# Two transformer blocks on one core: Silu gates taken together, keys and gated rows turned by DMA, softmax shifts formed in the maximum's own instruction

## The chip, the core and the metric

The kernel runs on one core of a Trainium2 chip. The core has a matrix engine (PE; its weight loads are listed as PEld), three engines for elementwise work (DVE, ACT, POOL), a queue engine (SP) that issues most DMAs, and 16 DMA engines. Each engine works through its own list in order, and waits on semaphores where an entry needs another engine's result. The metric is the device time of one execution in microseconds.

## The reference, cut to what matters

512 tokens of width 1024 pass through two blocks. In the second block 256 context rows give further keys and values.

```
# block 1
x = x + diff_attention(rmsnorm(x))      # 8 heads, two softmaxes each: p = softmax(s0) - lam*softmax(s1),
                                        # s = q.k - slope_h*distance, causal; 64 wide, q and k rms-normalised
x = x + hier_moe(rmsnorm(x))            # 16 experts, two per token inside one of four groups
# block 2
p = modulated_norm(x) @ w_in            # f_in, f_gate, q, k, v, na_gate: 512 columns each
y = real(fft2(f_in.reshape(512, 4, 128), axes=(tokens, channels))) / sqrt(512*128)
f = (y @ w_four) * silu(f_gate)
s = concat(q.k/8 + bias where the key is in the query's window, q.kc/8)     # kc: 256 context keys
n = softmax(s) @ concat(v, vc) * silu(na_gate)                              # q, k, kc rms-normalised, with gains
out = x + gate * (concat(f, n) @ w_out)
```

## The kernel before

Every product is done in fp16 as a high and a low part: `hilo` (L165) makes them, the high part by a Copy on ACT, the low one by a subtraction on DVE, and `mm3` (L155 in the rows) issues three matmuls for each product. Work on tokens is in four tiles of 128 rows. Apart from a start that is ordered by hand, a scheduler takes the program's instructions by priority (roughly: as written) as soon as its own model has their inputs ready, and so fixes each engine's list at build time. Buffers come from pools: eight PSUM banks (three "mm", two "tp", three "sc"), 18 large SBUF slots, five 1024-wide work buffers (`w4`), six 512-wide ones (`w2`).

The span has these stages (us from its start): 0 to 60 loads and the first norm; 60 to 262 projections and attention of block 1; 262 to 300 output projection and router; 300 to 580 the sixteen experts; 580 to 640 the context rows and block 2's norm; 640 to 712 the products of block 2 for k, v, q and the attention's gate (kx, vx, qx, ng), one after the other; 712 to 840 the neighbourhood attention with the Fourier branch between its pieces; 837 to 875 the product with w_out (z).

**Softmax, both blocks.** Scores of one query tile and head stand in a PSUM bank (s, ns). One DVE instruction adds the bias and reduces to the row's maximum (L508, L1423); a small DVE instruction multiplies the maximum by minus the scale (nmx L511: 64 times; nmxn L1426: 32 times); ACT takes Exp with that as its bias (L512, L1427).

**Turning.** Keys and queries are needed with channels on the partitions. `pairs_T` (L299) turns them by PE: transposes against the identity (L217, fp32) into a "tp" bank, then `hilo` with the gain. It does so for the context's keys (bank kcp, 8 transposes) and block 2's keys (kxp, 16), both called between the four products of vx, by `late.pop()`. Probabilities of the neighbourhood attention (`flip`) are split in SBUF and turned by `dma_start_transpose` on SP (L1436): 32 of them, from one half of two ring buffers to the other. SP takes DMAs in its list's order; an entry that waits holds all behind it.

**The Fourier branch.** `fourier()` (L1285) is a generator that `neighbours` advances at two points of each of its steps: `Fill(fourier(), 72)`. It computes u for the groups g = 0..3 (f_in, turned), folds each by DVE into f and fh/fl, multiplies by cosines and sines over the channels (`first(g)`: bank ab, evacuated to the tiles ab), then over the tokens (yp, yq: both "mm" banks), unfolds into yT, and then, tile by tile, the gate's product fg, its Silu, and `fouriered(t)`: y @ w_four (fo), times the gate (DVE, in fg), four transposes (fT) into cT. `first(g)` runs after the product u of g+1; `first(3)` right before the loop over yp and yq. The weights of w_out (bo) are loaded late in this branch. The attention's own turned result (nT) goes to the other half of cT.

Of the kernel before, what the change touches and what calls it, by code (L numbers as in the profile page):

```python
# [10 lines left out]
F16 = mybir.dt.float16  # L11
# [89 lines left out]
def block_kernel(ctx: ExitStack, tc: tile.TileContext, a, out, dbg=None):  # L101
# [74 lines left out]
    def S(name, i=0, n=1):  # L176
        lo = COLS[name][0]
        return sm[:, lo + i:lo + i + n]
# [140 lines left out]
    def proj_heads(ah, al, n, w, gain, th, tl, desc, nm, nxt, every, late, done=None, dense=False, pop=1):  # L319
        nats = []  # L320
        scale = []
        for t in range(n):
            if t % 2 == 0:
                pair = w4(f"{nm}nat{t}")
            nat = pair[:, (t % 2) * 512:(t % 2) * 512 + 512]
            ps = done[t] if done else (yield from project(ah, al, t, w.w, f"{nm}{t}", every=every, dense=dense, then=scale))
            while scale:
                scale.pop()()
            if t == pop and late:
                yield from late.pop()  # L330
            scale.append(heads_norm(ps, nat, f"{nm}{t}", desc))
            if nxt:
                nxt.piece(-(-4 // n))
            nats.append(nat)
            yield
        scale.pop()()
        late.append(pairs_T(nats, gain, th, tl, nm))
# [98 lines left out]
    nc.vector.tensor_scalar_mul(g2, S("q2g", 0, 2), 16.0)  # L436
    wog = const.tile([P, 1], F32, name="wog")
# [38 lines left out]
    def attention(hf, fill, last=None):  # L476
# [19 lines left out]
        def soft1(h, i):  # L496
            head = hf * 4 + h
            hsc = 2.0 ** -(head + 1) / MASTER0
            n = P * (i + 1)
            nm = f"{head}{i}"  # L500
            if i == 0:
                sums_h[h] = tiny.tile([P, 2, 4], F32, tag="sums", name="sums" + nm)
            sums = sums_h[h]
            pex = []
            for c, ps in enumerate(st[h, i]):
                z = w2(f"z{nm}{c}")
                mx = tiny.tile([P, 1], F32, tag="mx", name=f"mx{nm}{c}")
                nc.vector.tensor_tensor_reduce(out=z[:, :n], in0=ps[:, :n], in1=master[:, 384 - P * i:],  # L508
                                               scale=1.0, scalar=-3e38, op0=ALU.add, op1=ALU.max, accum_out=mx)
                nmx = tiny.tile([P, 1], F32, tag="nmx", name=f"nmx{nm}{c}")  # L510
                nc.vector.tensor_scalar(nmx, mx, -hsc, None, op0=ALU.mult)  # L511
                nc.scalar.activation(z[:, :n], z[:, :n], AF.Exp, bias=nmx, scale=hsc, accum_out=sums[:, c, i:i + 1])  # L512
                pex.append(z)
            st[h, i] = pex
# [705 lines left out]
    for f in kcn:  # L1220
        f()
# [9 lines left out]
    late.append(pairs_T([cnat[:, :512], cnat[:, 512:]], lambda j: g2[:, 1:2], kch, kcl, "kc"))  # L1231
# [4 lines left out]
    run_all(proj_heads(xh, xl, NT, W["k"], lambda j: g2[:, 1:2], kxh, kxl, D2, "kx", None, KD, late, None, True, 3))  # L1236
# [9 lines left out]
    for i, b in enumerate((1, 2, 3, 0)):  # L1246
        ps = bank("sc" if i % 2 else "mm", f"vx{b}")
        vw = W["v"].w
        for k in range(KD):
            bh, bl = (v[:, k, :] for v in xw) if b == 0 else (v[:, k, 128 * b - 64:128 * b + 64] for v in (xh, xl))  # L1250
            mm3(ps, bh, bl, vw[0][:, k, :], vw[1][:, k, :], k == 0, k == KD - 1)
        if i == 0:
            run_all(late.pop())
        hilo(vxh[:, b, :], vxl[:, b, :], ps, 1.0 / SW)
        W["q"].piece()
# [14 lines left out]
    _, cTh, cTl = hl_slots("cT")  # L1270
# [4 lines left out]
    def fourier():  # L1275
# [51 lines left out]
        yield from first(3)  # L1327
# [7 lines left out]
        for g in range(4):  # L1335
            pp_, pq = bank("mm", f"yp{g}"), bank("mm", f"yq{g}")
# [23 lines left out]
        def fouriered(t):  # L1360
# [6 lines left out]
            stt(fg[:, 512:], ps, D2, fg[:, :512], op1=ALU.mult)  # L1367
            yield
            pt = bank("tp", f"fT{t}")
            for k in range(4):  # L1370
                transpose_to(pt[:, k * P:(k + 1) * P], fg[:, 512 + k * P:512 + (k + 1) * P])
            hilo(cTh[:, 0:4, s], cTl[:, 0:4, s], pt.rearrange("p (k t) -> p k t", k=4), 4.0)

        for t in range(NT):
            ps = yield from project(xh, xl, t, W["fg"].w, f"fg{t}", every=2)
            fos[t] = w4(f"fg{t}")
            nc.scalar.activation(fos[t][:, :512], ps, AF.Silu, scale=D2)
            f4.piece()
            if t == NT - 1:
                W["o0"] = Weights(cols(a["w_out"], 0), "bo0")  # L1380
            yield
            if t > 0:
                yield from fouriered(t - 1)
        W["o0"].piece(2)
        yield from fouriered(3)
        W["o0"].piece(2)

# [3 lines left out]
    def neighbours(fill):  # L1391
# [15 lines left out]
        def soft(j, t):  # L1407
# [7 lines left out]
            for c in range(2):  # L1415
                nm = f"n{j}{t}{c}"
                m = nbm[c]
                if t != 2:
# [4 lines left out]
                nc.vector.tensor_tensor_reduce(out=z, in0=st[j, t][c], in1=m, scale=1.0, scalar=-3e38, op0=ALU.add,  # L1423
                                               op1=ALU.max, accum_out=mx)
                nmx = tiny.tile([P, 1], F32, tag="nmx", name="nmx" + nm)
                nc.vector.tensor_scalar(nmx, mx, -ISC, None, op0=ALU.mult)  # L1426
                nc.scalar.activation(z, z, AF.Exp, bias=nmx, scale=ISC, accum_out=sums[:, 2 * t + c:2 * t + c + 1])  # L1427
# [134 lines left out]
```

## Time and profile before

| | us |
|---|---|
| median of 3 runs | 874.3 (873.94, 874.3, 877.48) |
| profiled execution | 876.94 |
| its span on the engines | 875.1 |
| busy in the span: PE / DVE / ACT / POOL | 806.9 / 644.7 / 523.9 / 145.8 |
| mean granted PE clock (1 is full speed) | 0.971 |

PE is busy for 92% of the span, DVE for 74%, ACT for 60%. These are averages over stages of different kinds, and a busy PE is not PE at its peak. The profiled execution lies 1.84 us above its own span and 2.64 us above the median of the runs.

### The profile page before, as it was taken

What the parts mean: (1) busy time and instruction counts of PE and PEld (TensorE: products, weight loads), DVE (VectorE), ACT (ScalarE), POOL (GpSimd) and SP (SyncE); (2) the same over time, 40 slices, a digit from 0 to 9 for tenths busy, and PEclk for the clock granted to TensorE, in tenths of its full rate; (3) what the DMA queues carried; (4) which work ended last, traced back from release to release, by engine and by line L of the source; (5) the groups of instructions that cost most, each with busy time, mean ns of one, the idle gap of its engine ahead of it and who ended that gap; (6) DMA issues with size and microseconds to landing.
All of it is one profiled execution on the core that took longest, in us unless ns stands there. A gap on an engine that the chain in (4) does not pass through costs nothing. (4 is left out here: it accounts for less than half of the span.)

```text
span 875.1 us, 19152 instructions
## 1 busy us (share of the span) xinstructions
PE 806.9 (92%) x7986; PEld 509.6 (58%) x7986; DVE 644.7 (74%) x1204; ACT 523.9 (60%) x847; POOL 145.8 (17%) x130
## 2 busy tenths in 40 slices
PE   5999989999989799999999999889799999899998
PEld 3444445444435688788887887654454445544544
DVE  5756667677994798999999999947945347886732
ACT  6525435454773388888888869755343246687600
POOL 1240122000152400000000000016440203221000
PEclk9999999999999699999999999989899999899999
DMA  9964330446127569999999999917900018559712
GB/s 340 387 224 137 123 97 25 144 147 238 49 82 280 191 220 344 375 400 395 394 398 397 394 398 380 373 33 256 357 13 24 1 27 179 110 107 231 187 44 71
DMA packets 108043, 187.62 MB, mean 214 GB/s; under 512 B 37199, under 2 KB 37712, under 8 KB 107952
## 3 DMA queue, kind: packets, MB, share of 16 engines
q1 hardware_dynamic: 102176, 167.61, 56.3%
q0 software_dynamic: 3568, 12.45, 4.0%
q10 hardware_dynamic: 2208, 6.29, 1.8%
q8 instruction: 64, 1.05, 0.5%
q14 instruction: 27, 0.22, 0.1%
HBM read 165.37 MB, written 12.58 MB: 203 GB/s over the span
## 5 line engine op out<-in xcount | busy, mean ns | idle before, releaser
L155 PEld LDWEIGHTS <-hT 128*128 128x128 f16 x576 | 55.2, 99 | 66.6 <-issue 8.6
L155 PEld LDWEIGHTS <-xnT 128*128 128x128 f16 x456 | 44.8, 99 | 52.9 <-issue 4.7
L155 PEld LDWEIGHTS <-hx 128*96 128x96 f16 x384 | 47.0, 125 | 33.9 <-issue 2.2
L512 ACT ACTIVATE z<-z,nmx 128x128 f32<-128x128 f32 (+3 forms) x64 | 35.6, 557 | 46.3 <-DVE nmx L511 46.1
L955 POOL DMA_DIRECT2D y_d<-y x16 | 8.2, 513 | 262.0 <-ACT y L954 262.0
L155 PE MATMUL xgp<-se,XSh 128*128 128x96 f16 x512 | 48.3, 211 | 0.9 <-DVE se L886 0.9
L155 PE MATMUL xgp<-se,XSl 128*128 128x96 f16 x512 | 48.5, 211 | 0.2 <-issue 0.2
L155 PEld LDWEIGHTS <-XSh 128*128 128x128 f16 x512 | 45.6, 101 | 1.3 <-DVE se L886 1.0
L155 PEld LDWEIGHTS <-XSl 128*128 128x128 f16 x512 | 45.7, 101 | 0.3 <-issue 0.3
L508 DVE CUSTOM_DVE_ANT_0 z<-s,misc_a 128x128 f32<-128x128 f32 (+3 forms) x64 | 30.1, 481 | 4.7 <-PE s L155 4.5
L1420 POOL TENSOR_TENSOR late_b<-late_b,misc_b 128x256 f32<-128x256 f32 x24 | 19.3, 823 | 82.5 <-DVE mxn L1423 82.2
L155 PEld LDWEIGHTS <-cT 128*128 128x128 f16 x216 | 20.1, 99 | 20.5 <-DVE cT L163 0.4
L163 DVE SCALAR_TENSOR_TENSOR ring<-zn,ring 128x512 f16<-128x512 f32 x32 | 22.0, 711 | 12.0 <-ACT ring L1428 12.0
L1423 DVE CUSTOM_DVE_ANT_0 zn<-ns,late_b 128x512 f32<-128x512 f32 x32 | 21.0, 682 | 12.2 <-PE ns L155 11.7
L1427 ACT ACTIVATE zn<-zn,nmxn 128x512 f32<-128x512 f32 x32 | 22.8, 714 | 11.3 <-DVE nmxn L1426 11.3
L155 PEld LDWEIGHTS <-oT 128*128 128x128 f16 x192 | 17.6, 100 | 18.0 <-issue 2.0
L155 PE MATMUL y<-wo0s,oT 128*128 128x512 f16 x96 | 26.1, 380 | 0.7 <-DVE on L564 0.3
L155 PE MATMUL s<-kk,qk 64*128 64x128 f16 (+3 forms) x192 | 25.6, 300 | 0.1
L155 PE MATMUL y<-wo1s,oT 128*128 128x512 f16 x96 | 24.2, 394 | 1.2 <-ACT oT L166 0.7
L155 PE MATMUL k<-wk1s,hT 128*128 128x512 f16 x96 | 23.3, 380 | 1.6 <-DVE nmx L511 1.6
L166 ACT ACTIVATE pth<-pt 128x128 f16<-128x128 f32 (+3 forms) x32 | 13.7, 429 | 17.8 <-PE pt L217 17.7
L155 PE MATMUL v<-wv1s,hT 128*128 128x512 f16 x96 | 24.3, 394 | 0.0
(734 smaller groups left out, 2385.0 us busy)
## 6 DMA issues: line engine op xcount, KB each, us to landing
w_gate<-in_w_gate SPq DMA_DIRECT2D x32, 1024.0 KB, 11.5
w_up<-in_w_up SPq DMA_DIRECT2D x32, 1024.0 KB, 11.1
w_down<-in_w_down SPq DMA_DIRECT2D x32, 1024.0 KB, 12.0
ada<-in_w_ada SPq DMA_DIRECT2D x12, 1024.0 KB, 7.4
y_d<-y POOLq DMA_DIRECT2D x16, 384.0 KB, 6.7
wk<-in_da_w_in SPq DMA_DIRECT2D x4, 1024.0 KB, 13.5
wv<-in_da_w_in SPq DMA_DIRECT2D x4, 1024.0 KB, 10.0
wo<-in_da_w_out SPq DMA_DIRECT2D x4, 1024.0 KB, 7.0
```

The costliest lines, as they stand in the source:

```text
L155: nc.tensor.matmul(o, lhsT=lhsT, rhs=rhs, start=start, stop=stop)
L163: return nc.vector.scalar_tensor_tensor(o, in0, sc, in1, op0=op0, op1=op1)
L166: nc.scalar.activation(h, src, AF.Copy, scale=scale)
L508: nc.vector.tensor_tensor_reduce(out=z[:, :n], in0=ps[:, :n], in1=master[:, 384 - P * i:], scale=1.0, scalar=-3e38, op0=ALU.add, op1=ALU.m ...
L512: nc.scalar.activation(z[:, :n], z[:, :n], AF.Exp, bias=nmx, scale=hsc, accum_out=sums[:, c, i:i + 1])
L955: nc.gpsimd.dma_start(y_d[e * CAP:(e + 1) * CAP, :], y[:CAP, :])
L1420: nc.gpsimd.tensor_tensor(m[:, :256], pos[j, "b"][:, c * 256:(c + 1) * 256], mask[:, v:v + 256], op=ALU.add)
L1423: nc.vector.tensor_tensor_reduce(out=z, in0=st[j, t][c], in1=m, scale=1.0, scalar=-3e38, op0=ALU.add, op1=ALU.max, accum_out=mx)
L1427: nc.scalar.activation(z, z, AF.Exp, bias=nmx, scale=ISC, accum_out=sums[:, 2 * t + c:2 * t + c + 1])
```

## The change

Three edits go together.

1. *Softmax.* The reducing instruction multiplies by minus the scale and takes the minimum, so that it leaves the negated, scaled scores and their minimum, which is Exp's bias as it stands; Exp runs with scale -1. The 64 nmx and the 32 nmxn fall away.
2. *Keys of block 2.* The context's keys and the block's keys are normalised, split in SBUF (times 64) and turned by DMA: six DMA transposes on SP (2 of kcsp, 4 of the kxnat buffers) for 24 PE transposes and the eight evacuations of their banks. The k gain is multiplied into the q gain.
3. *Fourier branch.* `first(3)` is called after g = 1 of the loop over yp and yq. The four gate products are evacuated by a Copy; four Silus from SBUF are written after all of them, then `fouriered` for the four tiles. It splits the gated rows in SBUF and turns them by DMA into cT (4 DMA transposes on SP) instead of 16 PE transposes. The first half of w_out's weights is asked for after the fourth gate product is evacuated.

```
+    def turn(norm, nat, s, o):
+        def go():
+            norm()
+            hilo(s[:, :512], s[:, 512:], nat, 64.0)
+            nc.sync.dma_start_transpose(o, s)
+        return go
...
             scale.append(heads_norm(ps, nat, f"{nm}{t}", desc))
+            if turned is not None:
+                scale.append(turn(scale.pop(), nat, pair[:, 512:].bitcast(F16), turned[:, :, t * P:(t + 1) * P]))
...
-        late.append(pairs_T(nats, gain, th, tl, nm))
+        if turned is None:
+            late.append(pairs_T(nats, gain, th, tl, nm))
...
+    nc.vector.tensor_scalar(g2[:, 0:1], g2[:, 0:1], g2[:, 1:2], 1.0 / 64.0, op0=ALU.mult, op1=ALU.mult)
...
-                                               scale=1.0, scalar=-3e38, op0=ALU.add, op1=ALU.max, accum_out=mx)
-                nmx = tiny.tile([P, 1], F32, tag="nmx", name=f"nmx{nm}{c}")
-                nc.vector.tensor_scalar(nmx, mx, -hsc, None, op0=ALU.mult)
-                nc.scalar.activation(z[:, :n], z[:, :n], AF.Exp, bias=nmx, scale=hsc, accum_out=sums[:, c, i:i + 1])
+                                               scale=-hsc, scalar=3e38, op0=ALU.add, op1=ALU.min, accum_out=mx)
+                nc.scalar.activation(z[:, :n], z[:, :n], AF.Exp, bias=mx, scale=-1.0, accum_out=sums[:, c, i:i + 1])
...
-    for f in kcn:
-        f()
+    csp = w4("kcsp", F16)
+    for t, f in enumerate(kcn):
+        turn(f, cnat[:, t * 512:(t + 1) * 512], csp[:, t * 1024:(t + 1) * 1024],
+             kvc16[:, :2048].rearrange("p (m t) -> p m t", m=8)[:, :, t * P:(t + 1) * P])()
...
-    late.append(pairs_T([cnat[:, :512], cnat[:, 512:]], lambda j: g2[:, 1:2], kch, kcl, "kc"))
...
-        if i == 0:
-            run_all(late.pop())
         hilo(vxh[:, b, :], vxl[:, b, :], ps, 1.0 / SW)
...
-        yield from first(3)
...
         for g in range(4):
+            if g == 2:
+                yield from first(3)
             pp_, pq = bank("mm", f"yp{g}"), bank("mm", f"yq{g}")
...
             stt(fg[:, 512:], ps, D2, fg[:, :512], op1=ALU.mult)
+            src = fg[:, :512].bitcast(F16)
+            hilo(src[:, :512], src[:, 512:], fg[:, 512:], 4.0)
+            nc.sync.dma_start_transpose(cT[0].rearrange("p v k t -> p (v k) t")[:, :, s], src)
             yield
-            pt = bank("tp", f"fT{t}")
-            for k in range(4):
-                transpose_to(pt[:, k * P:(k + 1) * P], fg[:, 512 + k * P:512 + (k + 1) * P])
-            hilo(cTh[:, 0:4, s], cTl[:, 0:4, s], pt.rearrange("p (k t) -> p k t", k=4), 4.0)
...
-            nc.scalar.activation(fos[t][:, :512], ps, AF.Silu, scale=D2)
+            nc.scalar.activation(fos[t][:, :512], ps, AF.Copy, scale=D2)
             f4.piece()
-            if t == NT - 1:
-                W["o0"] = Weights(cols(a["w_out"], 0), "bo0")
             yield
-            if t > 0:
-                yield from fouriered(t - 1)
-        W["o0"].piece(2)
-        yield from fouriered(3)
-        W["o0"].piece(2)
+        W["o0"] = Weights(cols(a["w_out"], 0), "bo0")
+        for t in range(NT):
+            nc.scalar.activation(fos[t][:, :512], fos[t][:, :512], AF.Silu)
+        for t in range(NT):
+            yield from fouriered(t)
+            W["o0"].piece(1)
```

The scheduler decides what becomes of this on each engine. Three places follow; the numbers behind the names are buffers.

PE of the kernel before, where the scores (ns) of one attention step give way to the Fourier branch and `first(3)` comes next:

```order
L155 LDWEIGHTS qkx
L155 MATMUL ns_10658<-kvc,qkx 128x256
L155 LDWEIGHTS fh_10557
L155 MATMUL ab_10565<-late_b,fh_10557 128x128
L155 LDWEIGHTS fh_10557
L155 MATMUL ab_10565<-late_b,fh_10557 128x128
L155 LDWEIGHTS fh_10557
L155 MATMUL nyp_10578<-late_b,fh_10557 1x128
```

PE of the change at the same place, behind the same scores:

```order
L155 LDWEIGHTS qkx
L155 MATMUL ns_10358<-kvc,qkx 128x256
L155 LDWEIGHTS ab_9869
L155 MATMUL yp_10394<-dfts,ab_9869 128x257
L155 LDWEIGHTS ab_9869
L155 MATMUL yp_10394<-dfts,ab_9869 128x257
L155 LDWEIGHTS ab_9870
L155 MATMUL yp_10394<-dfts,ab_9870 128x257
L155 LDWEIGHTS ab_9869
L155 MATMUL yq_10395<-dfts,ab_9869 128x256
```

Where PE had the matmuls on fh, the last folded group, yp and yq of the first groups now stand, whose input is ab.

ACT of the kernel before, around the first gate Silu:

```order
L1427 ACTIVATE zn_10875,nsum_10865<-zn_10875,nmxn_10878 128x512
L1377 ACT_TABLE_LOAD
L1377 ACTIVATE fg_10927<-fg_10884 128x512
L1428 ACTIVATE ring_9997<-zn_10875 128x512
L1427 ACT_TABLE_LOAD
L1427 ACTIVATE zn_10957,nsum_10865<-zn_10957,nmxn_10960 128x512
```

ACT of the change, from the first gate's Copy (L1387) to the second's; Silu is L1392, Exp L1434, the Copy into the ring L1435:

```order
L1387 ACTIVATE fg_10737<-fg_10694 128x512
L1434 ACTIVATE zn_10767,nsum_10679<-zn_10767,mxn_10768 128x512
L1392 ACT_TABLE_LOAD
L1392 ACTIVATE fg_10737<-fg_10737 128x512
L1435 ACTIVATE ring_9844<-zn_10767 128x512
L1434 ACT_TABLE_LOAD
L1434 ACTIVATE zn_10773,nsum_10679<-zn_10773,mxn_10774 128x512
L1434 ACTIVATE zn_10857,nsum_10679<-zn_10857,mxn_10858 128x512
L1435 ACTIVATE ring_9844<-zn_10773 128x512
L1387 ACTIVATE fg_10821<-fg_10778 128x512
```

The first Silu stands between two Exps, with a table load on either side, ahead of the second gate's Copy. The whole list holds 15 table loads in either kernel.

SP of the change, late in the neighbourhood attention (L1381 turns the gated rows, L1443 the probabilities, L195 loads weights, L1501 loads the residual rows); the kernel before has no L1381 entry, and its bo loads stand further up among the ring's:

```order
L1443 DMA_TRANSPOSE ring_9843<-ring_9843 128x8x128
L1381 DMA_TRANSPOSE cT_9840<-fg_10737 128x8x128
L1443 DMA_TRANSPOSE ring_9843<-ring_9843 128x8x128
L195 DMA bo_11396<-in_w_out 128x4x512
L1381 DMA_TRANSPOSE cT_9840<-fg_10821 128x8x128
L195 DMA bo_11397<-in_w_out 128x4x512
L1381 DMA_TRANSPOSE cT_9840<-fg_10915 128x8x128
L1443 DMA_TRANSPOSE ring_9844<-ring_9844 128x8x128 x2
L1381 DMA_TRANSPOSE cT_9840<-fg_11009 128x8x128
L1501 DMA XR_11400<-x_d 128x1024 x2
```

The four new transposes stand between those of the ring, and each is followed by entries that wait for it to be issued.

## Rows read from the trace of the kernel before

**Rows 1.** Windows: stretch, length, busy per engine (instructions), PE clock, DMA share, GB/s.

```profile
60.00:262.00 202.00, 189.72 (x1212) 93.67 (x1211) 146.26 (x447) 105.88 (x237) 36.04 (x23) 0.99 0.34 115
258.00:262.00 4.00, 0.89 (x9) 0.59 (x10) 4.00 (x5) 0.00 (x0) 4.00 (x3) 1.00 0.96 359
640.00:712.00 72.00, 71.83 (x351) 34.73 (x350) 33.19 (x47) 27.49 (x41) 12.41 (x9) 1.00 0.03 8
712.00:840.00 128.00, 114.30 (x1085) 65.44 (x1083) 92.86 (x234) 86.97 (x159) 25.69 (x29) 0.95 0.65 147
776.00:812.00 36.00, 33.15 (x279) 17.45 (x277) 24.85 (x55) 30.77 (x49) 6.81 (x8) 0.95 0.83 204
```

**Rows 2.** Waits of PE, 612 to 875: total us, times, longest.

```profile
PE na L155 <- DMA ring<-ring: 6.0, 5, 1.9
PE ab L155 <- ACT fh L166: 4.1, 1, 4.1
...
PE fT L217 <- DVE fg L163: 2.7, 2, 2.1
```

**Rows 3.** Waits of ACT, 60 to 300.

```profile
ACT z L512 <- DVE nmx L511: 46.1, 23, 6.0
```

**Rows 4.** Groups by form, 60 to 300 (L511) and 712 to 840: busy us, mean ns, idle before.

```profile
L511 DVE TENSOR_SCALAR nmx<-mx 128x1 f32<-128x1 f32 x64 | 9.0, 145 | 0.2
...
L1426 DVE TENSOR_SCALAR nmxn<-mxn 128x1 f32<-128x1 f32 x32 | 4.0, 144 | 0.0
...
L1377 ACT ACT_TABLE_LOAD x4 | 5.1, 1283 | 0.1
```

**Rows 5.** Timeline of POOL before 262: start, us, what, idle before.

```profile
249.57 1.97 POOL L207 TENSOR_TENSOR or6r<-or6u,mhalf 128x4 f32<-128x4 f32 x1 [12.46 <-DVE nmx L511]
251.52 9.69 POOL L277 TENSOR_TENSOR w_gate0s<-w_gate,w_gate0s 128x1024 f16<-128x1024 f32 x4
```

**Rows 6.** Timeline of PE, 651 to 653.

```profile
651.31 1.04 PE L217 MATMUL kxp<-cst,kxnat 128*128 128x128 f32 x8
652.18 1.24 PE L155 MATMUL vx<-bvs,xnT 128*128 128x512 f16 x5
```

**Rows 7.** Timeline of PE, ACT and DVE around the wait for fh.

```profile
747.39 0.49 PE L155 MATMUL ns<-kvc,qkx 64*128 64x256 f16 x3
...
748.35 0.57 ACT L1311 ACTIVATE u<-u 128x512 f32<-128x512 f32 x1
...
749.44 0.69 DVE L163 SCALAR_TENSOR_TENSOR ab<-ab,ab 128x512 f16<-128x512 f32 x1 [0.19 <-ACT ab L166]
...
751.29 0.64 ACT L166 ACTIVATE fh<-f 128x513 f16<-128x513 f32 x1 [1.73 <-DVE f L1322]
...
751.98 0.39 PE L155 MATMUL ab<-late_b,fh 128*128 128x128 f16 x2 [4.10 <-ACT fh L166]
```

**Rows 8.** Windows behind the two waits.

```profile
752.00:756.00 4.00, 4.00 (x43) 3.07 (x44) 3.28 (x10) 2.14 (x6) 2.44 (x3) 0.50 0.30 71
...
802.00:804.00 2.00, 2.00 (x11) 0.85 (x9) 1.29 (x2) 1.97 (x5) 0.00 (x0) 0.50 0.45 123
```

**Rows 9.** Timeline, 795 to 802, around the first wait for fg.

```profile
795.07 1.28 ACT L1377 ACT_TABLE_LOAD   x1
796.36 0.60 ACT L1377 ACTIVATE fg<-fg 128x512 f32<-128x512 f32 x1
...
800.56 0.66 PE L217 MATMUL fT<-cst,fg 128*128 128x128 f32 x4 [2.09 <-DVE fg L163]
...
801.05 0.34 PE L155 MATMUL na<-vx,ring 128*128 128x64 f16 x6
```

**Rows 10.** SP's timeline, 715 to 720, and DMA issues, 712 to 840 (median us to landing).

```profile
717.51 2.73 SPq L1436 DMA_TRANSPOSE ring<-ring  x2
...
ring<-ring SPq DMA_TRANSPOSE x32, 3.4
```

More of the change, by code (lines that the diff above doesn't have):

```diff
@@ L317, in project, with proj_heads @@
         return ps
-    def proj_heads(ah, al, n, w, gain, th, tl, desc, nm, nxt, every, late, done=None, dense=False, pop=1):
+    def turn(norm, nat, s, o):
[4 more added lines that the diff above has]
+        return go
+    def proj_heads(ah, al, n, w, gain, th, tl, desc, nm, nxt, every, late, done=None, dense=False, pop=1, turned=None):
         nats = []
@@ L322, in proj_heads @@
         for t in range(n):
-            if t % 2 == 0:
+            if t % 2 == 0 or turned is not None:
                 pair = w4(f"{nm}nat{t}")
-            nat = pair[:, (t % 2) * 512:(t % 2) * 512 + 512]
+            nat = pair[:, :512] if turned is not None else pair[:, (t % 2) * 512:(t % 2) * 512 + 512]
             ps = done[t] if done else (yield from project(ah, al, t, w.w, f"{nm}{t}", every=every, dense=dense, then=scale))
@@ L1230, in block_kernel @@
     tail.close()
-    late.append(pairs_T([cnat[:, :512], cnat[:, 512:]], lambda j: g2[:, 1:2], kch, kcl, "kc"))
     qkx = [slot(f"{x}kx", F16).rearrange("p (v j t) -> p v j t", v=2, j=4) for x in "qk"]
     qxh, qxl, kxh, kxl = (x[:, v] for x in qkx for v in range(2))
-    run_all(proj_heads(xh, xl, NT, W["k"], lambda j: g2[:, 1:2], kxh, kxl, D2, "kx", None, KD, late, None, True, 3))
+    run_all(proj_heads(xh, xl, NT, W["k"], None, None, None, D2, "kx", None, KD, late, None, True,
+                       turned=qkx[1].rearrange("p v j t -> p (v j) t")))
     xw = w4("xw", F16).rearrange("p (v k t) -> p v k t", v=2, k=KD)
@@ L1267, in block_kernel @@
         nc.scalar.activation(ng[:, t, :], ps, AF.Silu, scale=D2)
-    _, cTh, cTl = hl_slots("cT")
+    cT, cTh, cTl = hl_slots("cT")
     dfg = lc[:, 1536:1792].bitcast(F16).rearrange("p (v n) -> p v n", v=2)
@@ L1422, in soft @@
                 mx = tiny.tile([P, 1], F32, tag="mx", name="mx" + nm)
[L1423 to L1427, printed above, removed]
+                nc.vector.tensor_tensor_reduce(out=z, in0=st[j, t][c], in1=m, scale=-ISC, scalar=3e38, op0=ALU.add,
+                                               op1=ALU.min, accum_out=mx)
+                nc.scalar.activation(z, z, AF.Exp, bias=mx, scale=-1.0, accum_out=sums[:, 2 * t + c:2 * t + c + 1])
                 nc.scalar.activation(ring[t % 2][:, 0, c, :512], z, AF.Copy, scale=256.0)
```

## The prediction

> **What bounds the kernel now.** I read the busy times by stage first. Through both attentions and the products PE leads: 189.72 of 202 us in 60 to 262, 71.83 of 72 in 640 to 712, 114.30 of 128 in 712 to 840 [rows 1]. There only two things count: less work on PE, and fewer of its idle stretches. The experts' stage between them is not touched by the change; it starts when the attention before it ends.
>
> Next come PE's waits in the last quarter: 4.1 us once for fh, 2.7 us twice for fg, 6.0 us five times for the ring's transposes [rows 2]. The reader is to see how few they are: a gain in the stage 712 to 840 is at most its 13.7 us of PE idle time, the transposes taken off PE, and what the clock gives back. The clock comes third: after each of the first two waits PE runs with a granted clock of 0.50 (1.2 of 2.4 GHz), all of 752 to 756 and all of 802 to 804 [rows 8]. A wait of 4.1 us was followed by 4 us of work at half speed, which is 2 us more.
>
> Last I asked who is late at these two waits. For fh it is the chain u (ACT, 748.35), the evacuation of ab, seven small DVE instructions, then fh at 751.29; PE, done with its scores at 747.88, sits until 751.98 [rows 7]. For fg it is ACT and DVE: a table load of 1.28 us, the Silu, then the product with fo on DVE, and PE's fT at 800.56 after 2.09 us [rows 9].
>
> **Softmax.** 96 small DVE instructions go, of 145 and 144 ns: 9.0 us in block 1 and 4.0 us in block 2 [rows 4]. DVE has room (146.26 of 202 us), so this is no bound lifted; what is gained is the delay on the chain maximum, Exp, sum, turned probabilities. ACT waited 23 times for nmx, 46.1 us in all [rows 3], but shortening each by 0.145 gives it 3.3 us, and PE is what counts. PE is idle for 12.3 us in 60 to 262, 3.1 of them in 258 to 262 [rows 1]. Bounds: nothing, if PE's other work fills the gaps already; 32 query steps by 0.145 us, 4.6 us, if every step waits for its chain. I take 2.0, since PE's busy share is 0.94 and the filler hides most.
>
> The rebuilt order also costs something here. Before, the row scale of the seventh head (or6r on POOL) ran at 249.57, ahead of four subtractions of 2.42 us each [rows 5]. In the new list two of these stand ahead of it. They wait for ACT's high parts, and DVE's scaled output (on6) waits for or6r with the last head's two maxima behind it. Bounds: nothing, if those high parts come early enough that both run in POOL's 12.46 us of idling; 4.85 us, if they start where they start now. The last head's chain already ends in a stretch in which DVE is 4.00 of 4.00 busy and PE only 0.89 [rows 1], so some would show. I take 1.0. Together: **-1.0** (from -4.6 to +4.9).
>
> **Keys by DMA.** The eight kxp transposes occupy PE from 651.31 to 652.18, 0.109 us each [rows 6]; 24 of them are 2.6 us, in a stage with 0.17 us of PE idle time. That is a firm gain unless a new wait appears. The keys are first read by the scores, after 712, and PE could turn them at 651.31, 60 us earlier; a transpose takes 1.37 us to issue and 3.4 to land [rows 10], six in a row under 29 us even if each waited for the one before. DVE and ACT have 33.19 and 27.49 of 72 us [rows 1], so the splits in SBUF cost nothing; without that cover they would be some 1.3 us each (0.57 for a Copy, 0.69 for a low part [rows 7]). The mask, the gate's and the Fourier branch's weights now stand behind transposes on SP, and a late mask delays a POOL addition that stands ahead of the last key tile's scale. I put that at nothing because the tile has the vx and qx products as cover; bound +3. Term: **-2.6** (from -2.6 to +0.4).
>
> **first(3) behind g = 1.** Where PE sat from 747.88 to 751.98, yp and yq of groups 0 and 1 now stand. They need ab of these groups, made earlier, and "mm" banks: one comes free when u is evacuated, at 748.92 (748.35 + 0.57), the other when ab's low part is done, at 750.13 [rows 7]. So yp can start about 3.0 us before the old end, and yq may wait some 0.7 more: 2.3 of the 4.1 us come back. The 2 us lost at half clock shrink with the wait; nothing in the rows says whether a shorter wait still lowers the clock, so 0 to 2.0, and I take 1.0. Term: **-3.3** (from -6.1 to 0, if the two banks come later than I read).
>
> **Gated rows by DMA.** Four fT take 0.49 us (800.56 to 801.05) [rows 9], sixteen 2.0. The waits for fg, 2.7 us [rows 2], go with them, since PE has nothing left that needs fg; of the clock's loss in 802 to 804, 1 us of work done in 2 [rows 8], I take 1.0. That is -5.7. Against it: four Copies of 0.60 us (as long as the Silu in [rows 9]) on ACT, which is busy 30.77 of 36 us in 776 to 812 [rows 1]; ACT's share there is so near PE's 33.15 that I count all 2.4. And SP: each new transpose holds the queue 1.37 us, and the ring's transposes, for which PE waits 6.0 us now, stand behind. Bounds nothing and 19.1 (below); I take 1.5, a quarter of four issues. The 32 nmxn off the ring's chain give back 0.5 of their 4.0. Term: -5.7 + 2.4 + 1.5 - 0.5 = **-2.3**.
>
> **The four Silus.** They are written together, but the lists keep 15 table loads, and the first Silu still stands between two Exps, with a load on either side. The loads take 1283 ns each [rows 4], and the Silu starts right behind (795.07 + 1.28, then 796.36) [rows 9]. So I count no load saved.
>
> The Trainium skill ("ScalarE: Activation LUTs", section "Table sets: the hidden batching unit") says to batch activations by table set, since a load comes with each change of set. This would speak for the edit, had the scheduler kept it; as the lists stand, the rule gives what I count, nothing. Its price of about 2.66 us for a load with its drain ("What ACT_TABLE_LOAD costs") is not what these rows show, which have 1.28 and no gap behind.
>
> **Sum.** -1.0 - 2.6 - 3.3 - 2.3 = -9.2 us. The profiled execution took 876.94, so 867.7; it lies 2.64 above the median of the runs, so the forecast is **865.1**.
>
> **Rivals.** (a) *Everything comes back*: both waits go with all of their clock loss, and the ACT copies and SP's issues hide. Then the third term is -6.1, the fourth -2.0 - 2.7 - 1 - 0.5 = -6.2: sum -15.9, time 858.4. For it: the waits are isolated, and PE has work queued. Against: ACT's load in 776 to 812. Chance 0.20.
>
> (b) *ACT absorbs the branch*: the Fourier stage keeps its length because the eight loads around the four Silus stay, 10.3 us, and 2.4 us of copies are added, so that terms three and four end at 0. Then 876.94 - 3.6 - 2.64 = 870.7; with the full POOL delay of 3.9 more, 874.6. For it: ACT's 30.77 of 36. Against: ACT is busy for only 86.97 of 128 us over the whole stage. Chance 0.21.
>
> (c) *Slower: SP's queue*. If each cT transpose waits for DVE's split, and the ring's transposes behind it wait for its 1.37 us of issue and its 3.4 of landing, PE's next na waits 4.77 us four times: 19.1 in place of the 1.5 counted, 882.7. It decides from 3.8 us exposed per transpose on: 4 by 3.8 less 1.5 is the way from 865.1 to 878.7. Against: values run two steps behind scores, which covers most of one landing. Chance 0.08.
>
> (d) *The Silus do end up in one stretch* on the chip's ACT, so that six of eight loads go: 6 by 1.283 is 7.7 us of ACT, and 857.4 if ACT set the pace. The lists, which are fixed at build, speak against it: 0.02. The section of the Trainium skill named above would then hold, and by its price the gain would be 16 us.
>
> My own case keeps 0.49, between 861 and 869.9.
>
> **Numbers.** A measurement of this kernel tells no change from one under about 0.5%, 4.4 us. Faster (under 869.9): 0.49 + 0.20 + 0.02 and a little of (b), 0.72; same (869.9 to 878.7): 0.20; slower: 0.08. The range of 8 in 10 is 856 to 874: below it, part of (a) with more softmax gain; above it, (c) and the end of (b).
>
> **What would show it.** Softmax: 64 and 32 small instructions missing on DVE, and PE idle in 60 to 262 down from 12.3 by 1 to 2; or6r late and on6 waiting for it if POOL costs. Keys: 640 to 712 shorter by 2.6 with PE still without gaps; a wait of PE for kx or kvc at the scores would show it wrong. first(3): yp within about a us of the scores' end, and no half clock behind. Gated rows: no wait for fg, na's waits for the ring near 6 us; well over 10 would be rival (c). ACT: a table load on either side of each Silu, each still 1.28. The prediction is wrong above all if the stage 712 to 840 is not shorter by some 5 us.

## The result and the profile after

The changed kernel took 862.99 us in the median of four runs (861.49 to 864.25), beside 874.52 for the kernel before (four runs): ratio 0.9871, 95% interval 0.9836 to 0.9906, so 8 to 14 us less. The forecast was 865.1 in a range of 856 to 874. The profiled execution took 863.25 us, 13.7 less than the profiled one before, with a span of 861.5. Runs of one kernel differ by 3 to 4 us in these two series, and by up to 13 in the longest one (the kernel before, 33 runs, 869.3 to 882.0). A second series of the changed kernel, below, gave 0.9892 (0.9863 to 0.9921), 9.0 us less.

The totals of the page first.

```profile
span 861.5 us, 18995 instructions
...
PE 796.8 (92%) x7946; PEld 504.6 (59%) x7946; DVE 638.6 (74%) x1107; ACT 523.9 (61%) x849; POOL 142.9 (17%) x130
```

PE lost 10 us of busy time, DVE 6; ACT kept its 523.9 exactly. PE's waits from 700 to the end are the answer to [rows 2]:

```profile
PE na L155 <- DMA ring<-ring: 3.5, 3, 2.3
PE yq L155 <- DVE ab L163: 1.6, 1, 1.6
PE ns L155 <- DVE mxn L1432: 1.2, 1, 1.2
PE gB L155 <- DVE fg L163: 1.0, 1, 1.0
PE na L155 <- ACT yt L1357: 0.6, 1, 0.6
PE yp L155 <- ACT u L1321: 0.6, 1, 0.6
```

The waits for fh (4.1) and for fT's input (2.7) are gone. The five small ones that stand for them sum to 5.0 us, and the ring's fell from 6.0 to 3.5. One of the five is still a wait for DVE's work on fg: gB, the spread of the last gate over the partitions, waits 1.0 us for it.

Where the time went is read best from the products that every kernel has. The view of one tile's instructions gives the first and last start of its group, as for the keys' and the gate's products, of before and of after:

```profile
L155 PE MATMUL kx<-bks,xnT x96: 379/379/634, 615.4 to 644.8; 128*128 128x512 f16 x96
...
L155 PE MATMUL ng<-ngws,xnT x96: 379/379/379, 689.6 to 712.1; 128*128 128x512 f16 x96
```

```profile
L155 PE MATMUL kx<-bks,xnT x96: 379/379/634, 614.7 to 642.9; 128*128 128x512 f16 x96
...
L155 PE MATMUL ng<-ngws,xnT x96: 379/379/379, 684.6 to 707.1; 128*128 128x512 f16 x96
```

From the last kx to the last ng it was 67.3 us and is 64.2. The same differences of starts for all runs are the table on which the rest goes. "scores" is the first product ns, and each stretch ends at the last product of its name; the ratio is to the kernel before on the same chip.

| kernel | scores to u | u to yq | yq to fo | fo to z | scores to z | ratio (95%) |
|---|---|---|---|---|---|---|
| before | 32.0 | 24.1 | 46.1 | 55.0 | 157.2 | |
| changed | 29.7 | 19.5 | 44.0 | 55.4 | 148.6 | 0.9871 (0.9836 to 0.9906) |
| changed_again | 29.7 | 19.9 | 47.6 | 55.7 | 152.9 | 0.9892 (0.9863 to 0.9921) |
| softmax_only | 29.7 | 23.1 | 44.8 | 54.6 | 152.2 | 0.9934 (0.9909 to 0.9958) |
| shift2_only | 29.7 | 22.4 | 45.0 | 55.6 | 152.7 | 0.9898 (0.9860 to 0.9935) |
| keys_only | 30.7 | 25.5 | 44.5 | 56.8 | 157.5 | 0.9932 (0.9907 to 0.9957) |
| first_only | 30.6 | 26.8 | 48.4 | 56.4 | 162.2 | 0.9995 (0.9967 to 1.0023) |
| rows_only | 30.6 | 24.4 | 39.6 | 59.1 | 153.7 | 0.9944 (0.9920 to 0.9969) |
| first_back | 29.7 | 22.1 | 39.6 | 55.8 | 147.2 | 0.9844 (0.9801 to 0.9886) |
| wide_silu | 29.7 | 19.9 | 40.3 | 55.4 | 145.3 | 0.9820 (0.9784 to 0.9855) |
| no_copy | 29.8 | 19.4 | 44.5 | 55.6 | 149.3 | 0.9883 (0.9844 to 0.9922) |
| rows_by_pe | 29.7 | 19.5 | 48.8 | 56.0 | 154.0 | 0.9933 (0.9905 to 0.9962) |
| wide_first_back | 29.7 | 21.7 | 39.6 | 55.5 | 146.5 | 0.9839 (0.9805 to 0.9872) |
| wide_shift2 | 29.7 | 21.4 | 39.5 | 55.8 | 146.4 | 0.9841 (0.9808 to 0.9874) |

Each stretch is from one profiled execution. The stretch from the first to the last step of block 1's attention, which five of these kernels share with before unchanged, lay between 179.7 and 182.2 in them and at 182.8 in before, so that differences of 3 us there mean nothing. In the last stage some figures repeat far better (29.7 nine times), but yq to fo does not: the changed kernel itself has 44.0 in one profile and 47.6 in the other, and with it 148.6 and 152.9 from scores to z.

Two places of the changed kernel answer to [rows 7, 9]. In its timeline, PE behind the scores:

```profile
740.41 0.49 PE L155 MATMUL yp<-dfts,ab 128*128 128x257 f16 x3 [0.55 <-ACT u L1321]
742.48 0.49 PE L155 MATMUL yq<-dfts,ab 128*128 128x256 f16 x3 [1.57 <-DVE ab L163]
...
745.00 0.34 PE L155 MATMUL na<-vx,ring 128*128 128x64 f16 x6 [0.61 <-ACT yt L1357]
```

yp starts when u has been evacuated, yq when ab has, as read from [rows 7]; the granted clock stays at 1.00 through 740 to 746. But some 20 us later a wait stands that before did not have: the chain of work, then SP's timeline (start, us).

```profile
758.79 0.60 DVE cT L163
759.39 0.23 DVE yt L163
759.62 6.94 DMA ring<-ring
766.56 0.05 issue
766.60 0.82 PE na L155 x12
```

```profile
757.23 1.24 SPq L1443 DMA_TRANSPOSE ring<-ring  x1
758.51 0.58 SPq L195 DMA_DIRECT2D bo<-in_w_out  x1
759.62 1.76 SPq L1443 DMA_TRANSPOSE ring<-ring  x1
761.45 0.63 SPq L195 DMA_DIRECT2D bo<-in_w_out  x1
```

The transpose issued at 759.62 lands 6.94 us later; the median is 3.3. The 1 MB load of w_out went out 1.1 us ahead of it. PE waits 2.27 us for it, from 764.33 on; with the median landing, by estimate, the transpose would have been there at 762.9, and PE would not have waited. The granted clock falls behind that wait (the window 766 to 768 has 0.50, the next 0.68):

```profile
764.00:766.00 2.00, 0.33 (x12) 0.21 (x8) 2.00 (x5) 2.00 (x5) 1.00 (x1) 0.96 1.23 229
766.00:768.00 2.00, 1.40 (x14) 0.92 (x15) 2.00 (x5) 1.97 (x4) 0.00 (x0) 0.50 1.05 359
768.00:770.00 2.00, 2.00 (x8) 0.78 (x7) 1.54 (x4) 1.98 (x3) 0.00 (x0) 0.68 1.19 312
```

The DMA share is above 1 in all three windows (1.05 to 1.23): the load and the transposes run at the same time.

### The profile page after: what moved, and what is told of

The parts are those of the page before. It is cut to its first block, busy times and chain, and to the rows that moved or that the text cites. A ratio compares the mean times of both kernels' runs of the same rounds, so it can differ in the third digit from the quotient of the medians.

```text
span 861.5 us, 18995 instructions
## 1 busy us (share of the span) xinstructions
PE 796.8 (92%) x7946; PEld 504.6 (59%) x7946; DVE 638.6 (74%) x1107; ACT 523.9 (61%) x849; POOL 142.9 (17%) x130
## 3 DMA queue, kind: packets, MB, share of 16 engines
q8 instruction: 64, 1.05, 0.5%
## 5 line engine op out<-in xcount | busy, mean ns | idle before, releaser
L155 PEld LDWEIGHTS <-hT 128*128 128x128 f16 x576 | 55.7, 100 | 67.6 <-issue 10.2
L155 PEld LDWEIGHTS <-xnT 128*128 128x128 f16 x456 | 44.8, 99 | 53.6 <-issue 3.8
L522 ACT ACTIVATE z<-z,mx 128x128 f32<-128x128 f32 (+3 forms) x64 | 35.5, 556 | 43.7 <-DVE mx L520 41.8
L155 PE MATMUL xgp<-se,XSl 128*128 128x96 f16 x512 | 48.4, 211 | 0.0
L520 DVE CUSTOM_DVE_ANT_0 z<-s,misc_a 128x128 f32<-128x128 f32 (+3 forms) x64 | 29.8, 482 | 5.9 <-PE s L155 5.9
L155 PEld LDWEIGHTS <-oT 128*128 128x128 f16 x192 | 17.0, 98 | 21.4 <-issue 4.2
L1434 ACT ACTIVATE zn<-zn,mxn 128x512 f32<-128x512 f32 x32 | 22.9, 715 | 10.9 <-DVE mxn L1432 10.8
L1432 DVE CUSTOM_DVE_ANT_0 zn<-ns,late_b 128x512 f32<-128x512 f32 x32 | 20.8, 680 | 11.5 <-PE ns L155 11.5
L166 ACT ACTIVATE pth<-pt 128x128 f16<-128x128 f32 (+3 forms) x32 | 13.8, 431 | 22.4 <-PE pt L217 22.2
L155 PE MATMUL kx<-bks,xnT 128*128 128x512 f16 x96 | 23.1, 398 | 0.3 <-ACT xnT L166 0.3
## 6 DMA issues: line engine op xcount, KB each, us to landing
w_down<-in_w_down SPq DMA_DIRECT2D x32, 1024.0 KB, 11.3
```

The source lines that it names most:

```text
L155: nc.tensor.matmul(o, lhsT=lhsT, rhs=rhs, start=start, stop=stop)
L166: nc.scalar.activation(h, src, AF.Copy, scale=scale)
L522: nc.scalar.activation(z[:, :n], z[:, :n], AF.Exp, bias=mx, scale=-1.0, accum_out=sums[:, c, i:i + 1])
L1434: nc.scalar.activation(z, z, AF.Exp, bias=mx, scale=-1.0, accum_out=sums[:, 2 * t + c:2 * t + c + 1])
```

## The experiments

**Each edit alone, on the kernel before.** *softmax_only* has edit 1.

```
-    ... op0=ALU.add, op1=ALU.max, accum_out=mx);  nmx = mx * -hsc;  Exp(bias=nmx, scale=hsc)
+    ... scale=-hsc, op0=ALU.add, op1=ALU.min, accum_out=mx);        Exp(bias=mx, scale=-1.0)
```

> The kernel before with the softmax edit alone (both blocks). Theory: the edit shortens a chain that PE waits for seldom; the span falls by 1 to 2 us up to the end of the attention of block 1, and PE's 2.1 us of waiting for the ring near 737 falls away, since the ring's rows are ready 0.14 us earlier per maximum; sum 870 to 873 us. The fh wait (4.1 us) and the fg waits (2.7 us) stay. Rival: the removed instructions were hidden, and the row scale of the seventh head, now behind two subtractions on POOL, gives the gain back: within 1 us of before, and the ring's wait near 737 stays, so that its loss in the changed kernel comes from another part.

Measured: 870.93 us, ratio 0.9934. The last stage is 5.0 us shorter, more than the theory had for the whole; 1.4 of that is in the first stretch also without the edit (30.6 in first_only and rows_only against 32.0), so 3.6 to 5.0 are the edit's. The fh wait fell to 3.0 us, and the ring's wait near 737 went, though one of 4.2 us for the ring came near 821, where before has 1.9. In block 1 nothing can be told from the spread.

*shift2_only* has edit 1 in the neighbourhood attention alone (the 32 nmxn).

```
 # soft(j, t) of neighbours() as changed; soft1 of block 1 as before
```

> The kernel before with the softmax edit in the neighbourhood attention alone (32 instructions). Theory: nearly all that the softmax edit gave alone (ratio 0.9934, with the stage from the first scores to the end 5.0 us shorter in its trace) comes from here: ratio 0.993 to 0.996, this stage 3 to 5 us shorter. Rival: it comes from block 1, whose maxima are twice as many; then this run is within 1 us of before.

Measured: 868.12 us, ratio 0.9898; scores to z 152.7. The theory holds for the place: block 2's 32 instructions carry the edit (3.1 to 4.5 us of the stage, counted as above); the ratio lies below its 0.993 to 0.996. ACT's wait for the maxima, 11.3 us for nmxn before, is 10.7; that is not where the gain shows. It shows in part in PE's waits for the ring, 6.0 us in five before and one of 3.8 now, and for fh, 2.5:

```profile
PE na L155 <- DMA ring<-ring: 3.8, 1, 3.8
...
PE ab L155 <- ACT fh L166: 2.5, 1, 2.5
```

Against these 3.8 us less stand waits that before did not have, 1.6 us for fg's evacuation and 1.1 in place of 0.2 for yt, so that PE's waits fall by 1.3 us in all. The work lost to the clock, counted as for *first_only* below, falls from 5.8 to 4.2 us. How the rest of the gain comes about is not shown.

*keys_only* has edit 2.

```
-        late.append(pairs_T(nats, gain, th, tl, nm))
+        scale.append(turn(...))    # norm, split in SBUF, dma_start_transpose
```

> The kernel before with the keys turned by DMA alone. Theory: 24 transposes leave PE in a stage without gaps, so the stretch from the first kx product to the last ng product is 2.6 us shorter, and nothing else moves: 871.5 to 872.5 us. Rival: the trace of the change shows this stretch 4.3 us shorter, so more than the transposes is saved (the weights behind the SP queue's loads, or gaps at the switches between fp32 and fp16 matmuls): 870 to 871 us.

Measured: 870.16 us, ratio 0.9932. From the last kx to the last ng it takes 64.2 us in its trace; 67.3 in before, softmax_only, shift2_only and rows_only alike. That is 3.1 us for 24 transposes, 0.13 each, near the theory's 2.6. From the first kx, as the expectation had it, it is 4.5 us, the rival's size; but the other 1.4 are the kx products (28.0 us in place of 29.4), which also take 28.0 without the edit (softmax_only) and 29.4 with it (rows_by_pe). The times say more, 4 to 8 us, and lie with the rival's 870 to 871. Ahead of this stretch the trace has another 2.4 us: the first kx starts at 613.0, in place of 615.4. But it starts at 611.2 and 612.4 in rows_only and first_only, which do not have this edit, so I leave the surplus open.

*first_only* moves the call of first(3).

```
-        yield from first(3)
 ...
         for g in range(4):
+            if g == 2:
+                yield from first(3)
```

> The kernel before with only the call of first(3) moved behind g = 1. Theory: the wait for fh (4.1 us) and the half clock behind it (2.2 us from 750.96 to 756.5) go; two waits for banks of 0.6 and 1.6 us come in their place: the stretch from the last u product to the last yq product is 3.5 to 4.5 us shorter, 870 to 871 us in all. Rival: the gain of 4.6 us in this stretch of the changed kernel needs the shorter softmax chain as well; alone it brings 2.3 us or less, 872 us or more.

Measured: 875.95 us, ratio 0.9995, and the last stage 5.0 us longer. The rival holds, and the stretch from u to yq, for which the move was made, is even 2.7 us longer (26.8 against 24.1): the fh wait is gone, but PE waits 1.7 us for u, 1.2 and 0.9 for yt, 2.8 for fg, and the clock is low for longer than before. Windows of this run:

```profile
746.00:748.00 2.00, 1.53 (x18) 1.18 (x16) 2.00 (x10) 0.90 (x2) 1.03 (x2) 0.50 0.76 145
748.00:750.00 2.00, 2.00 (x19) 0.97 (x16) 2.00 (x9) 0.93 (x2) 1.42 (x2) 0.50 0.04 8
750.00:752.00 2.00, 2.00 (x12) 1.02 (x11) 0.43 (x1) 2.00 (x6) 0.00 (x0) 0.50 0.39 131
760.00:762.00 2.00, 2.00 (x18) 1.43 (x19) 1.60 (x2) 0.71 (x2) 0.00 (x0) 0.50 1.03 345
762.00:764.00 2.00, 1.53 (x8) 0.83 (x7) 1.51 (x6) 1.93 (x4) 0.00 (x0) 0.50 1.56 201
```

Summed over windows of 2 us from 708 on (PE's busy time times what the clock lacks to 1), 12.4 us of work were lost to the clock here, 5.8 from 712 on in before, with 13.9 and 14.7 us of idle time up to the last product z.

*rows_only* has the end of edit 3: Copies, Silus, turning by DMA, and the earlier request for the first half of w_out.

```
-            nc.scalar.activation(fos[t][:, :512], ps, AF.Silu, scale=D2)
+            nc.scalar.activation(fos[t][:, :512], ps, AF.Copy, scale=D2)
 ...
+            nc.sync.dma_start_transpose(cT[0].rearrange("p v k t -> p (v k) t")[:, :, s], src)
```

> The kernel before with only the end of the Fourier branch changed: Copies, Silus written together, gated rows turned by DMA. Theory: sixteen transposes (2.0 us) and the waits for fg (2.7 us) leave PE, four Copies (2.4 us) come to ACT, the table loads stay at fifteen: 870 to 873 us. Rival (SP's queue): the ring's transposes wait behind the four new ones, PE's waits for the ring go from 6 to over 10 us, and the time is 874 us or more.

Measured: 870.45 us, ratio 0.9944. The theory's size is right. The stretch yq to fo falls by 6.5 us, fo to z gives 4.1 back. The waits of fT for fg went, but gB now waits 2.0 us for DVE's work on fg. The rival on SP's queue fails: the ring's waits fell to 2.7 us in five, and the new transposes land in 3.2 us in the median (one of the four took 7.1):

```profile
ring<-ring SPq DMA_TRANSPOSE x32, 3.3
...
cT<-fg SPq DMA_TRANSPOSE x4, 3.2
```

**One edit undone.** *first_back* is the changed kernel with first(3) at its old place.

```
+        yield from first(3)
 ...
-            if g == 2:
-                yield from first(3)
```

> The changed kernel with first(3) called where it was before, all else as changed. Theory: moving it is worth what the changed kernel gained between the last u and the last yq product, so without it the wait for fh (3 to 5 us) with half clock behind it comes back and this stretch, 19.5 us, becomes 23 to 24: 866 to 867 us. Rival, after the run with this move alone, which showed no gain (ratio 0.9995) and half clock in two places: the move is worth nothing or costs, the stretch owes its gain to the shorter softmax chain, and this kernel takes 860 to 863 us.

Measured: 860.22 us, ratio 0.9844. The rival holds: without the move the kernel is no slower, and the last stage is 1.4 us shorter than in the changed kernel's first profile, 5.7 than in its second. u to yq is longer by 2.2 to 2.6 us, as the step had it, but yq to fo is 39.6 in place of 44.0 and 47.6. The fh wait is 2.5 us here, not 4.1, since the other edits already shortened its chain. On SP the first two loads of w_out go out together from 759.00 on, and the next transpose of the ring follows only 5 us later:

```profile
756.78 1.83 SPq L1442 DMA_TRANSPOSE ring<-ring  x1
759.00 0.92 SPq L195 DMA_DIRECT2D bo<-in_w_out  x2
763.95 10.54 SPq L1442 DMA_TRANSPOSE ring<-ring  x5
```

*changed_again* is the changed kernel once more, on the chip of rows_by_pe, wide_first_back and wide_shift2.

> The changed kernel itself, beside the three below on the same chip, since the kernel before varied by several us between the runs of different calls. Both theories: a ratio of 0.984 to 0.990 to the kernel before. What it decides is the place of the others: if first_back's 0.9844 was the chip's doing, this one comes out near 0.985 too, and the move of first(3) is worth nothing either way; if it stays near 0.987 or above, the move costs 1 to 3 us.

Measured: 866.48 us, ratio 0.9892, which by the rule set above points to a cost of the move of first(3); but the intervals of 0.9892 and 0.9844 overlap, so the times do not settle it. Its profile has the stall of the first one again, larger. The chain there, and SP's entries:

```profile
760.96 8.77 DMA ring<-ring
769.73 0.05 issue
769.78 0.82 PE na L155 x12
```

```profile
759.85 0.58 SPq L195 DMA_DIRECT2D bo<-in_w_out  x1
760.96 2.69 SPq L1443 DMA_TRANSPOSE ring<-ring  x1
```

The transpose takes 8.77 us to land, PE waits 4.2, and yq to fo is 47.6.

*no_copy* drops the four Copies.

```
-            nc.scalar.activation(fos[t][:, :512], ps, AF.Copy, scale=D2)
+            nc.scalar.activation(fos[t][:, :512], ps, AF.Silu, scale=D2)
 ...
-            nc.scalar.activation(fos[t][:, :512], fos[t][:, :512], AF.Silu)
```

> The changed kernel with each Silu straight from PSUM, as before, in place of Copy and Silu; the gated products, their transposes and the loads of w_out stay where the change put them. Theory: four Copies of 0.59 us leave ACT, the table loads stay at 15, and the time is within 1 us of the changed kernel or 1 to 2 us below: 861 to 863 us. Rival: the Copies free a PSUM bank sooner than a Silu behind a table load would, so without them the gate products wait for banks and the stretch of the gate products is 2 to 4 us longer: 865 to 867 us.

Measured: 865.28 us, ratio 0.9883; scores to z 149.3, yq to fo 44.5. The time lies in the range that the rival named, but its mechanism does not show: the stretch is not longer than the changed kernel's 44.0 and 47.6, and PE has no wait for the banks of the gate products. The ratio stands between the 0.9871 and 0.9892 of the changed kernel's two series, some 1 us from either, so no cost of the Copies shows.

*rows_by_pe* turns the gated rows by PE again, in the change's order.

```
-            hilo(src[:, :512], src[:, 512:], fg[:, 512:], 4.0)
-            nc.sync.dma_start_transpose(...)
+            transpose_to(pt[:, k * P:(k + 1) * P], fg[...]);  hilo(cTh[:, 0:4, s], cTl[:, 0:4, s], pt, 4.0)
```

> The changed kernel with the gated rows turned by PE again (16 transposes, evacuated from PSUM), all else as changed: Copies, Silus and products with fo stay where the change put them. Theory: the DMA turning as such is worth the 2.0 us of PE work and part of the waits for fg; ratio 0.2 to 0.5% above the changed kernel's, the stretch from the last yq to the last fo product 2 to 4 us longer. Rival: the gain of this part comes from the new order (all products with fo after the four gate products), not from the turning; then this kernel is within 1 us of the changed one.

Measured: 870.62 us, ratio 0.9933, beside 0.9892 on the same chip: 0.4% above, with intervals that overlap. Both profiles have a ring wait of 4.2 us, so they can be compared: yq to fo is 1.2 us longer. That is between theory and rival: less than the 2.0 us of the transposes' PE work. It speaks for the rival's view that the larger part of the 6.5 us that rows_only won in this stretch belongs to the order, though the medians, 4.1 us apart, speak for the theory. Its chain has a ring transpose that lands as late as in changed_again:

```profile
757.47 8.90 DMA ring<-ring
```

**The Silus truly together.** *wide_silu* writes the four Copies side by side and takes one Silu.

```
-            nc.scalar.activation(fos[t][:, :512], fos[t][:, :512], AF.Silu)      # four times
+        nc.scalar.activation(gates, gates, AF.Silu)                               # [128, 2048]
```

> The changed kernel with the four Copies written into one 2048-wide buffer and one Silu over it, which can't be split: 9 table loads in the list in place of 15, on either side of one Silu. Theory: ACT is near PE's pace in this stage, so six loads (7.7 us of ACT) and three instructions' start-up bring 2 to 5 us between the first gate product and the last na product: 858 to 861 us. Rival: ACT was off the path there, since no row of PE's waits names it for more than 0.6 us; within 1 us of the changed kernel, or slower, because the gates' products with fo now all wait for the last gate and four turned rows come in one burst.

Measured: 860.45 us, ratio 0.9820. Its groups from 708 to 840 have three table loads, where the changed kernel has nine:

```profile
L1432 ACT ACT_TABLE_LOAD x2 | 2.6, 1283 | 0.0
...
L1390 ACT ACTIVATE gates<-gates 128x2048 f32<-128x2048 f32 x1 | 1.9, 1910 | 0.0
...
L1390 ACT ACT_TABLE_LOAD x1 | 1.3, 1283 | 0.0
```

The gain is of the theory's size, but not by its mechanism, as the next run shows: here too the loads of w_out moved, to 769.38 behind four transposes that SP starts from 758.52 on, and PE's wait for the ring is 0.9 us in all. A transpose follows the load by 1.1 us here as well, and the two that start from 770.49 on land 6.1 and 7.5 us later; but PE has gate products to do meanwhile (SP's timeline, then the ring's landings from 770 to 773):

```profile
769.38 0.58 SPq L195 DMA_DIRECT2D bo<-in_w_out  x1
770.49 4.96 SPq L1441 DMA_TRANSPOSE ring<-ring  x2
```

```profile
DMA to landing us min/median/max: 6.1/6.8/7.5
```

*wide_first_back* has the wide Silu and first(3) at its old place.

```
+        yield from first(3)                      # ahead of the loop, as before
+        nc.scalar.activation(gates, gates, AF.Silu)
```

> The one wide Silu together with first(3) at its old place, the rest as changed. Theory: the two gains seen in the traces of the last stage (3.6 us for the wide Silu, 1.7 us for first(3) back) touch different stretches and add: 5 us below the changed kernel on the same chip, ratio 0.979 to 0.982. Rival: they are paid by the same slack of DVE and ACT before the gate products, so that the sum is no more than the wide Silu's 3.6 us.

Measured: 861.25 us, ratio 0.9839. The rival holds: the gains do not add. Against first_back the six loads fewer (7.7 us of ACT) are worth 0.7 us in the last stage (146.5 against 147.2) and nothing that the times resolve. What wide_silu and first_back had in common was a stretch yq to fo without the ring's stall.

*wide_shift2* keeps block 1's softmax as before on top of that.

```
 # soft1 of block 1 as before; the rest as in wide_first_back
```

> As the kernel with the wide Silu and first(3) back, but with the softmax edit in the neighbourhood attention alone; block 1 keeps its nmx instructions, and or6r stands ahead of the subtractions on POOL again. Theory: in block 1 the edit brought 0 to 1 us and cost as much by or6r's place (PE's waits there sum to 14 us with it and 11 to 12 without), so this kernel is within 1.5 us of its neighbour, rather below. Rival (the forecast's): the 64 shorter chains are worth 1 to 2 us, and this kernel is that much slower.

Measured: 860.87 us, ratio 0.9841 beside 0.9839: block 1's 64 instructions are worth nothing that can be measured, as the theory had it. Both this kernel and wide_first_back are faster than the changed kernel on the same chip by 5.2 to 5.6 us in the median. First_back (0.9844), wide_silu (0.9820) and these two cannot be told apart by their intervals; by the medians each of the four would be a better version to keep than the changed kernel. Between wide_silu and wide_first_back the move of first(3) shows neither gain nor cost.

## Why the prediction was right, point by point

The time and its direction came out as forecast, 11.5 us less (9.0 in the second series) where 9.2 were summed. That the sum fits so well is partly luck. The terms for softmax (with the 0.5 for nmxn), keys, first(3) and the gated rows were 1.5, 2.6, 3.3 and 1.8 us; alone, the parts took 5.5, 6.3, 0.5 and 6.0 us off the median, 18 in all, and together they give about half of that. Three parts were sized too low, first(3) too high, and the parts do not add.

**Keys by DMA, -2.6: right in the stretch that it names.** 3.1 us after kx; the larger gain of the times is open. The cover held: PE has no wait for kx or kvc.

**Softmax: the place was wrong.** Block 1 was to give -1.0 net and gives nothing measurable. The POOL delay came as the list said: or6r ran at 253.52, against 249.57 [rows 5], and PE waited 2.7 us for the last z (1.3 in the trace before), but no stretch of block 1 is longer by more than the spread. PE's idle time in 60 to 262, which was to fall by 1 to 2 us, rose from 12.3 to 14.9:

```profile
60.00:262.00 202.00, 187.15 (x1218) 93.56 (x1216) 144.93 (x385) 105.91 (x237) 35.65 (x23) 0.99 0.38 127
```

Block 2's nmxn, for which I took 0.5 of their 4.0 us, give 3.1 to 5.0 in the last stage. The step that failed is the sizing of these 32 by DVE's time. In shift2_only PE's waits for the ring and for fh, which stand behind DVE's queue, are shorter by 2.2 and 1.6 us; 2.5 us of other waits come in their place, and 1.6 us less is lost to the clock. That the waits are the whole cause is argued and not shown.

**first(3), -3.3: right where it stands beside the other edits, wrong alone and in sum.** In the changed kernel the stretch u to yq is 2.2 to 2.6 us shorter than with first(3) at the old place, with the two bank waits that I read (0.55 and 1.57) and no half clock. On the kernel before (first_only) the same move makes it 2.7 us longer, with the clock at 0.50 from 746 to 752: the term needs the other edits, which the prediction did not make a condition. And in the changed kernel the next stretch is 4 to 8 us longer. I followed the four cT transposes on SP and gave no price to the other thing that edit 3 moves on that queue, the load of w_out's first half, which now comes 24 us earlier, counted from the first scores (758.51 less 707.4, where it was 787.60 less 712.4). The part of SP's list shown with the change does not reach so far up; it has the third and the fourth load only. The kernel before has, on SP:

```profile
787.60 0.56 SPq L195 DMA_DIRECT2D bo<-in_w_out  x1
788.73 1.25 SPq L1436 DMA_TRANSPOSE ring<-ring  x1
```

With first(3) behind g = 1 the first load goes out right ahead of a ring transpose that PE needs: the first two loads stand behind 15 and 16 of the ring's 32 transposes (21 and 22 in the kernel before). That the load delays the transpose is read from the traces: in both profiles of the changed kernel, in no_copy and in rows_by_pe the ring transpose that PE then waits for follows a w_out load by 1.1 us, and yq to fo is 44.0 us or more; in the five kernels with the branch's new end whose loads stand elsewhere in SP's list (both behind the 16th in rows_only and first_back, behind the 18th and the 20th in the three with the wide Silu) it is 39.5 to 40.3. Right behind a load a transpose lands late in all of the last three too (5.7 to 7.5 us), but PE waits for the ring there for 1.2 us in all at most. What costs, as far as these traces tell, is that the 16th transpose, between the two loads, is the one that PE needs next. A kernel with only that load moved was not run, so the cause is argued from the order and not shown by itself.

**Gated rows, -2.3: right in size.** Alone, 2.1 to 3.5 us of the last stage (1.4 of it lies between the scores and u, ahead of the edit). fT's waits for fg went; that PE has nothing left that needs fg was wrong, since gB then waits 1.0 us for it (2.0 in rows_only). For ACT's 2.4 us of Copies, which I charged in full, no cost shows (no_copy). For SP's 1.5 us none shows at the four new transposes; 2.3 and 4.2 of the ring's 3.5 and 6.4 us in the two profiles stand at the other entry.

**The four Silus, 0: right.** Nine loads stood in the stage, as the lists said.

```profile
L1434 ACT ACT_TABLE_LOAD x5 | 6.4, 1283 | 0.1
L1392 ACT ACT_TABLE_LOAD x4 | 5.1, 1283 | 0.1
```

The Trainium skill ("ScalarE: Activation LUTs", section "Table sets: the hidden batching unit") asks for batches by table set. The wide Silu obeys it, and the loads do go from nine to three, as the rule says. The six loads, 7.7 us of ACT, were worth 0.7; from 700 on no wait of PE for ACT in the changed kernel is over 0.6 us, which fits.

Of the rivals, (a) fails by the clock, which is still at 0.50 behind the ring's wait; (b)'s mechanism by no_copy and by the 0.7 us of the six loads, though its outcome, terms three and four at nothing, is not excluded: the last stage is 8.6 us shorter in one profile and 4.3 in the other, of which the softmax edit alone gives 3.1 to 5.0; (c) by the ring's waits of 3.5 and 6.4 us in all, though its queue did bite at another entry; (d) by the load count.

## What to carry to other kernels

When an edit lets a large load go out earlier, look in the order at which small transfer on the same queue comes right behind it, and who waits for that one. Do not size a removed instruction by its own duration alone, but look at the waits of the bounding engine that stand behind its queue: 32 of them, 4.0 us on an engine with room, were worth 3.1 to 4.5 us of the stage. And when edits are made together, run each alone and each undone: here one part, which looked good where it stood, lost more in the next stretch of the traces than it gained, by 1.4 and 5.7 us in the last stage of two profiles.

## What the runs showed that was not expected

A transpose by DMA that lands in 3.3 us in the median took 6.9 us (twice, no_copy's too), 8.8 and 8.9 us when a 1 MB load had been issued 1.1 us ahead of it. Two that followed such loads by some 5 us, in rows_only and first_back, landed in 3.1 and 3.7. And idle time alone does not tell what the clock takes: first_only, with many short waits, was idle for as long as before, while the work lost at the lower clock doubled, 12.4 against 5.8 us.
